# Tokens loaded by a matmul with a diagonal of norm factors, and 24 transposes of the identity as the tensor engine's first work

## The chip, the cores and the metric

The kernel runs on one core of a Trainium2 chip. Its engines are PE (matmul; PEld is the loading of the stationary operand), DVE (vector), ACT (activation), POOL and SP, which here only issues transfers. Each engine works through its own instructions strictly in the order in which they stand in the program. The metric is device time in microseconds of one launch, lower is better. The profile is one other execution, recorded by the hardware profiler.

## The reference

One step of a one-layer decoder over 1024 prompt tokens and 32 sample tokens (8 sequences of 4), width 1024, all in float32:

```python
def rmsnorm(x, g):
    return x * rsqrt(mean(x * x) + 1e-6) * g

def trunk_layer(x):
    x = x + 0.5 * rmsnorm(swiglu(rmsnorm(x, g[0])), g[1])       # FFN 1, inner width 2816
    h = rmsnorm(x, g[2]); z = h @ w_in                          # mLSTM q,k,v,o,i,f and window attention q,k,v
    u = concat(mlstm_heads(z), window_attention(z))
    x = x + rmsnorm(u @ w_out, g[3])
    x = x + 0.5 * rmsnorm(swiglu(rmsnorm(x, g[4])), g[5])       # FFN 2
```

The outputs are x for prompt and sample, and the new caches and states. The change concerns what comes before and at the first products of FFN 1: loading x, its norm and transposition.

## The kernel before, in words

**Tiling.** Tokens lie in four quarters q = 0 to 3, each 256 prompt tokens and 8 sample tokens (QW = 264 columns). The width of 1024 lies in eight blocks of 128 partitions, two to a tile (kp = 0 to 3). A float32 product is made of three matmuls in the type float32r: each operand is split into a high part (ACT rounds: `wh`, `Xh`) and a low part (DVE subtracts: `wl`, `Xl`), and high x high, high x low and low x high are summed. One such matmul has a 128x128 stationary operand and 264 moving columns.

**Stages.** FFN 1: the first pair of inner blocks goes plainly, quarter by quarter (PSUM tiles `pl`); the other ten pairs by a scheme with fewer products (`gu`) that needs sums and differences of the normed x of two quarters (function `sums`: tiles `xt`, then splits). Then the down projection (`pd`), first for quarters 0 and 1, then for 2 and 3; then the mix stage (`pz`, `pv`, `po`, `pw`), FFN 2 likewise, and the output.

**The start** (`load_x`). For each quarter SP loads 256 rows of tokens (`xt`, tokens on partitions). The sum of squares of each token (`jk`, `xss`) gives by `rstd`, ten small DVE instructions, the factor `r`. PE transposes the 16 blocks of 128x128 (`xT`, PE's transpose against the identity), ACT copies them to `xr`, POOL adds the 8 sample columns. A product of `r`, broadcast over 128 partitions, with the identity (`rb`) makes a row of factors `rrow` on all partitions. DVE multiplies `xr` by gain and `rrow` (`xb`, in `blocks`), and `Xh`/`Xl` are split from that. The unnormed `xr` is stashed in DRAM (`xs`) for the residual.

**The residual** (`post`). After the down projection of a pair of quarters the stashed tiles are loaded again (`x<-xs`). The sum of squares of the result is made by DVE (`sq`) and three matmuls with ones (`cs`); `rstd` and `rb` make the row `cr`; DVE multiplies and adds (`y`), ACT and DVE split for the next stage (`xh`, `xl`). PE goes on with the down projection of quarters 2 and 3 meanwhile. PSUM tiles for `cs` and `rb` share one single bank (BANKS `c=1`): `rb` of quarter 0 can be written only when DVE has read `cs` of quarter 1.

**Order.** The code spawns generators with due times in units of PE's estimated time (`Order`, the tables XW, XQ, PQ, SUMS), and a list scheduler then sets the order on each engine. So an edit at one place moves instructions at others.

## Time and profile before

| what | value |
|---|---|
| runs | 2020.64 us median of 3 (2015.86 to 2020.72) |
| the profiled execution: own time, span | 2019.21 us, 2017.4 us |
| mean granted TensorE clock in it | 0.996 |
| PE busy | 1986.5 us, 98% of the span |
| DVE, ACT, POOL busy | 1168.4, 874.9, 35.6 us |
| first `pl` matmul; first `gu` matmul | 17.01 us; 78.82 us after the span's start |

A row of a timeline has start, duration, engine, line, instruction, and in brackets how long the engine had been idle and what ended that. A row of instructions merged into one ("x4") has the time from the first start to the last end. Matmuls overlap, so what one costs is read from the distance of two starts, not from its duration. A float32 matmul (not float32r) shows as two records. The granted clock (PEclk) is a share of full speed.

### The profile page before, as it was taken

Reading aid. Unit: us, or ns where it says so; the run is one execution under the profiler, and the core shown is the slowest. Engines: PE = TensorE matmul, PEld = TensorE weight load, DVE = VectorE, ACT = ScalarE, POOL = GpSimd, SP = SyncE. Lnnn points to the kernel's source line nnn. Section 1 sums busy time; section 2 is a strip of 40 time slices with the busy share of each in tenths; the row PEclk is TensorE's granted clock in tenths of the full one; section 3 lists DMA queues with packets and bytes.
Section 4 is the critical chain, followed back from the end, with each engine's and each line's share of the span. In section 5 each row is a group of like instructions: output and inputs, shape, how many; then the busy total and the mean of one; then the engine's idle time right before and its main releaser. Section 6 shows DMA issues by size and latency. Waiting matters only on the chain.

```text
span 2017.4 us, 40347 instructions
## 1 busy us (share of the span) xinstructions
PE 1986.5 (98%) x16178; PEld 1942.6 (96%) x16178; DVE 1168.4 (58%) x2822; ACT 874.9 (43%) x2087; POOL 35.6 (2%) x166
## 2 busy tenths in 40 slices
PE   7999999999999999999999999999999999999997
PEld 7999999999999999987999999999999999999997
DVE  5855555557238436467556758785555556534764
ACT  6533333336336332346244655353333334533553
POOL 0000000000000001100101000000000000000000
PEclk9999999999999999999999999999999999999999
DMA  6122222226346343201214143322222223545773
GB/s 234 65 85 77 90 69 74 76 95 177 108 142 208 104 102 124 68 1 38 68 53 134 57 133 116 108 78 82 65 84 80 91 64 120 167 129 162 226 223 116
DMA packets 279690, 216.66 MB, mean 107 GB/s; under 512 B 21032, under 2 KB 252640, under 8 KB 279488
## 3 DMA queue, kind: packets, MB, share of 16 engines
q1 hardware_dynamic: 279504, 214.11, 35.0%
q8 instruction: 126, 2.06, 0.5%
q14 instruction: 60, 0.49, 0.1%
HBM read 172.39 MB, written 42.49 MB: 107 GB/s over the span
## 4 chain that ended last, share of the span: by engine, by line
PE 91%; DVE 3%; DMA 3%; ACT 2%; issue 1%; SPq 0%; DVEq 0%; ACTq 0%
PE gu L154 41%; PE pd L154 23%; PE pz L154 7%; PE pw L154 4%; PE pl L154 4%; PE pv L154 3%; PE po L154 2%; DMA raw<-ffn_w_down 2%; PE cs L154 1%; PE rb L154 1%; PE swo L154 1%; PE sws L154 1%; PE E L154 1%; ACT wh L196 1%; PE swp L151 1%
## 5 line engine op out<-in xcount | busy, mean ns | idle before, releaser
L154 PE MATMUL gu<-Xh,wh 128*128 128x264 f32 x2240 | 636.6, 284 | 0.0
L154 PE MATMUL gu<-Xl,wh 128*128 128x264 f32 x2240 | 636.0, 284 | 0.0
L154 PE MATMUL gu<-Xh,wl 128*128 128x264 f32 x2240 | 635.1, 284 | 0.0
L197 DVE TENSOR_TENSOR wl<-raw,wh 128x512 fp32r<-128x512 f32 x458 | 301.6, 670 | 384.3 <-ACT wh L196 376.5
L154 PE MATMUL pd<-hq,wh 128*128 128x264 f32 x2816 | 520.8, 286 | 0.1
L196 ACT CAST wh<-raw 128x512 fp32r<-128x512 f32 x458 | 270.1, 602 | 459.4 <-PE pd L154 193.2
L154 PEld LDWEIGHTS pd<-hq,wh 128*128 128x128 f32 x2816 | 437.8, 189 | 0.4 <-ACT yo L853 0.4
L154 PEld LDWEIGHTS gu<-Xh,wh 128*128 128x128 f32 x2240 | 421.1, 188 | 0.5 <-ACT sc L752 0.2
L154 PEld LDWEIGHTS gu<-Xh,wl 128*128 128x128 f32 x2240 | 421.6, 188 | 0.0
L154 PEld LDWEIGHTS gu<-Xl,wh 128*128 128x128 f32 x2240 | 421.3, 188 | 0.0
L154 PE MATMUL pd<-hq,wl 128*128 128x264 f32 x1408 | 401.1, 285 | 0.0
L154 PEld LDWEIGHTS pd<-hq,wl 128*128 128x128 f32 x1408 | 265.4, 188 | 0.2 <-DVE wl L197 0.2
L752 ACT COPY sc<-gu 128x264 f32<-128x264 f32 x240 | 91.0, 380 | 272.2 <-PE gu L154 268.0
L197 DVE TENSOR_TENSOR wl<-ws,wh 128x512 fp32r<-128x512 f32 x160 | 108.8, 690 | 87.6 <-ACT wh L196 84.7
L763 DVE TENSOR_TENSOR h<-gu,sc 128x264 f32<-128x264 f32 x120 | 51.8, 432 | 102.2 <-PE gu L154 83.3
L154 PE MATMUL pz<-xh,wh 128*128 128x264 f32 x352 | 102.3, 291 | 0.6 <-DVE z L1684 0.6
L154 PE MATMUL pz<-xh,wl 128*128 128x264 f32 x352 | 100.8, 286 | 0.0
L154 PE MATMUL pz<-xl,wh 128*128 128x264 f32 x352 | 100.5, 285 | 0.0
L196 ACT CAST wh<-ws 128x512 fp32r<-128x512 f32 x160 | 95.9, 623 | 4.1 <-PE pl L154 2.5
L764 ACT ACTIVATE h<-h 128x264 f32<-128x264 f32 x120 | 50.9, 425 | 106.5 <-DVE h L763 106.5
L769 DVE TENSOR_TENSOR sc<-gu,sc 128x264 f32<-128x264 f32 x120 | 51.6, 432 | 56.8 <-PE gu L154 51.4
L154 PE MATMUL pl<-Xh,wh 128*128 128x264 f32 x256 | 72.9, 299 | 3.3 <-ACT Xh L196 2.1
(368 smaller groups left out, 2969.6 us busy)
## 6 DMA issues: line engine op xcount, KB each, us to landing
raw<-ffn_w_down SPq DMA_DIRECT2D x80, 512.0 KB
raw<-ffn_w_gate SPq DMA_DIRECT2D x44, 512.0 KB
raw<-ffn_w_up SPq DMA_DIRECT2D x44, 512.0 KB
h<-h SPq DMA_DIRECT2D x80, 264.0 KB
hq<-h SPq DMA_DIRECT2D x160, 132.0 KB
raw<-ffn_w_down SPq DMA_DIRECT2D x40, 384.0 KB
x<-xs SPq DMA_DIRECT2D x48, 264.0 KB
raw<-w_in SPq DMA_DIRECT2D x21, 512.0 KB
```

Source lines behind the costliest of these rows:

```text
L151: K.nc.tensor.transpose(out, lhsT, rhs)
L154: K.nc.tensor.matmul(out, lhsT, rhs, start=start, stop=stop, **kw)
L196: K.nc.scalar.copy(hi, src)
L197: (eng or K.nc.vector).tensor_tensor(lo, src, hi.bitcast(F32), op=ALU.subtract)
L752: nc.scalar.copy(sc[n][:, g], ps)
L763: nc.vector.tensor_tensor(d, bk[tg, g], sc[n][:, g], op=ALU.add)
L764: nc.scalar.activation(d, d, AF.Silu)
L769: nc.vector.tensor_tensor(sc[n][:, g], src, sc[n][:, g], op=ALU.add)
```

## The change

- `load_x` no longer transposes against the identity. The factors `r` are computed first, DVE writes them as a diagonal (`diagonal`: identity times `r`, two of 128x128 for a quarter, in the tile `C`), and PE multiplies each block of tokens by the diagonal: transposition and norm in one float32 matmul. ACT makes `Xh` from PSUM with the gain as scale, DVE makes `Xl` from PSUM, ACT copies the normed x without gain (`xn`), and this is what is stashed.
- `rstd` gets its first guess by one instruction instead of two, and can also return the root `ru`. `rb` now broadcasts the root, and `post` of FFN 1 multiplies the reloaded tiles by it (16 new DVE instructions).
- `sums` makes the gained tiles `xb` (16 by DVE, 16 by ACT) that it used to find ready.
- The sample tokens come first and have their own norm; POOL copies 48 small pieces instead of 16.
- The first weights (`w0`) come in eight tiles of 256 KB between the tokens of quarters 0 and 1, and quarter 0's first products go over kp outermost (`first_pair`) with four PSUM tiles open.
- 24 transposes of the identity stand ahead on PE, one activation ahead on ACT.
- The copies of the attention caches from DRAM to DRAM become stores out of the tiles `kc` and `vc`, in `swa_sample`.

The core of the diff:

```diff
-XW = [2.0, 0.15, 0.2]
+XW = [2.0, 0.15, 4.0]
-XQ = [0, 0.0, 4.0, 10.0]
+WARM = 24
+XQ = [0, 3.0, 10.0, 20.0]
-SUMS = {(2, 0, 0): 0, (3, 0, 0): 1}
+SUMS = {1: {(1, 1, 1): 0, (3, 0, 0): 1}, 3: {(2, 0, 0): 0, (3, 0, 0): 1}}
...
+def first_loads(K):
+    K.xt = [slot(K, "xt")[0:32, 0:512] for _ in range(2)]
+    for i in range(2):
+        nc.sync.dma_start(K.xt[i], A["x_sample"].rearrange("b t d -> (b t) d")[:, i * 512:(i + 1) * 512])
+    load_tokens(K, 0)
+    for kp in range(4):
+        for mat, n in enumerate(("ffn_w_gate", "ffn_w_up")):
+            K.w0[kp, mat] = slot(K, "w0")[:, 0:512].rearrange("p (k m) -> p k m", k=2)
+            nc.sync.dma_start(K.w0[kp, mat], A[n][0, 0].rearrange("(k p) m -> p k m", p=P)[:, 2 * kp:2 * kp + 2, 0:256])
+    load_tokens(K, 1)
...
-    ri = r.bitcast(I32)
-    nc.vector.tensor_scalar(ri, v.bitcast(I32), 1, None, op0=ALU.arith_shift_right)
-    nc.vector.tensor_scalar(ri, ri, -1.0, float(0x5F3759DF), op0=ALU.mult, op1=ALU.add)
+    nc.vector.tensor_scalar(r.bitcast(I32), v.bitcast(I32), -0.5, float(0x5F3759DF), op0=ALU.mult, op1=ALU.add)
...
+    nc.vector.tensor_tensor(u, v, r, op=ALU.mult)
+    return r, u
...
+def diagonal(K, r, w, i):
+    d = K.C[0:w, i, 0:w]
+    K.last = K.nc.vector.tensor_scalar(d, K.ident[0:w, 0:w], r, None, op0=ALU.mult).ins
+    return d
...
-                pe(K, ps[:, (2 * i + j) * P:(2 * i + j + 1) * P], t[k // 4][:, (k % 4) * P:(k % 4) * P + P], K.ident,
-                   tr=True)
-        nc.scalar.copy(pair(x[kp])[:, :, 0:2 * P], ps.rearrange("p (a t) -> p a t", a=2))
+                pe(K, ps[:, (2 * i + j) * P:(2 * i + j + 1) * P], t[k // 4][:, (k % 4) * P:(k % 4) * P + P], dg[j])
+        for i in range(2):
+            nc.scalar.activation(h2[:, i, 0:2 * P], ps[:, i * 2 * P:(i + 1) * 2 * P], AF.Copy,
+                                 scale=K.gain[:, 2 * kp + i:2 * kp + i + 1])
+        for i in range(2):
+            ins = nc.vector.scalar_tensor_tensor(l2[:, i, 0:2 * P], ps[:, i * 2 * P:(i + 1) * 2 * P],
+                                                 K.gain[:, 2 * kp + i:2 * kp + i + 1], h2[:, i, 0:2 * P].bitcast(F32),
+                                                 op0=ALU.mult, op1=ALU.subtract)
+        nc.scalar.copy(x2[:, :, 0:2 * P], ps.rearrange("p (a t) -> p a t", a=2))
...
+        if phase == 1:
+            nc.vector.tensor_tensor(pair(t), pair(t), K.r[q].unsqueeze(1).to_broadcast([P, 2, QW]), op=ALU.mult)
...
+    nc.scalar.activation(warm, K.ones, AF.Silu)
+    for i in range(WARM):
+        nc.tensor.transpose(ps[:, 0:P], K.ident, K.ident)
```

What the scheduler makes of it stands below at three places. `xT` are the PSUM tiles of transposed tokens, `rb` the broadcast row; `xt`, and `raw` for quarter 1 now, hold loaded tokens; `C` holds the diagonals; numbers are the program's own.

PE at the start of the program, before: quarter 0's transposes need only the tokens, and the `rb` product comes ahead of the first `pl`.

```order
L151 MATMUL gps_94<-ident,graw_91 128x52
L151 MATMUL xT_146<-ident,xt_98 128x128
L151 MATMUL xT_146<-ident,xt_102 128x128
L151 MATMUL xT_146<-ident,xt_98 128x128
L151 MATMUL xT_146<-ident,xt_102 128x128
L151 MATMUL xsT_152<-ident,xt_106 128x32 x4
```

PE at the same place now:

```order
L158 MATMUL gps_132<-ident,graw_95 128x52
L1928 MATMUL warm_136<-ident 128x128 x24
L161 MATMUL xsT_186<-C,xt_98 128x32 x4
L161 MATMUL xsT_186<-C,xt_99 128x32 x4
L161 MATMUL xT_228<-C,xt_102 128x128
L161 MATMUL xT_228<-C,xt_104 128x128
```

The token blocks moved behind the diagonals, that is behind the sums of squares and `rstd`.

DVE before quarter 1's diagonals now (`ru_374` is its root, `C` the two diagonals; this had no counterpart before, since quarter 1's transposes waited for nothing of DVE's):

```order
L204 TENSOR_TENSOR wl_483<-w_15_122,wh_482 128x512
L273 TENSOR_SCALAR v_371<-xsn_369 128x2
L204 TENSOR_TENSOR wl_499<-w_16_124,wh_498 128x512
L274 TENSOR_SCALAR r_372<-v_371 128x2
L338 MEMSET xss_704 128x6
L409 SCALAR_TENSOR_TENSOR Xl_282<-xT_276,gain,Xh_281 128x256 x2
L276 TENSOR_TENSOR rt_373<-r_372,v_371 128x2
L277 TENSOR_TENSOR rt_373<-rt_373,r_372 128x2
L278 SCALAR_TENSOR_TENSOR ru_374<-rt_373 128x2
```

Here two weight splits and quarter 0's last `Xl` stand between the steps of quarter 1's `rstd`; six more rows follow before `C`. The rows of PE that need them stand in the midst of quarter 0's products:

```order
L161 MATMUL pl_338<-Xl_266,wh_352 128x264
L161 MATMUL rb_568<-ident,ru_374 128x128
L161 MATMUL xT_387<-C,raw_126 128x128
L161 MATMUL xT_387<-C,raw_127 128x128
L161 MATMUL xT_387<-C,raw_126 128x128
```

Whatever stands behind these rows on PE follows them in time, quarter 0's remaining products too.

DVE where `post` of quarters 0 and 1 begins, in the down projection of FFN 1, before (`sq` with one operand is the fold ahead of `cs`; `v` is the first step of `rstd`):

```order
L508 TENSOR_TENSOR sq_6367<-sq_6367,sq_7563 128x528
L197 TENSOR_TENSOR wl_7741<-raw_7738,wh_7740 128x512
L197 TENSOR_TENSOR wl_7745<-raw_7738,wh_7744 128x512
L244 TENSOR_TENSOR sq_6363<-sq_6363 128x264
L244 TENSOR_TENSOR sq_6367<-sq_6367 128x264
L197 TENSOR_TENSOR wl_7807<-raw_7804,wh_7806 128x512
L197 TENSOR_TENSOR wl_7811<-raw_7804,wh_7810 128x512
L265 TENSOR_SCALAR v_7851<-cs_7846 128x3
```

DVE at the same place now:

```order
L204 TENSOR_TENSOR wl_7875<-raw_7868,wh_7874 128x512
L516 TENSOR_TENSOR x_7917<-x_7917,rrow_439 128x528
L516 TENSOR_TENSOR x_7920<-x_7920,rrow_439 128x528
L516 TENSOR_TENSOR x_7923<-x_7923,rrow_439 128x528
L251 TENSOR_TENSOR sq_6493<-sq_6493 128x264
L204 TENSOR_TENSOR wl_7941<-raw_7938,wh_7940 128x512
L204 TENSOR_TENSOR wl_7945<-raw_7938,wh_7944 128x512
L516 TENSOR_TENSOR x_7972<-x_7972,rrow_572 128x528
L516 TENSOR_TENSOR x_7975<-x_7975,rrow_572 128x528
L516 TENSOR_TENSOR x_7978<-x_7978,rrow_572 128x528
L516 TENSOR_TENSOR x_7981<-x_7981,rrow_572 128x528
L273 TENSOR_SCALAR v_7989<-cs_7984 128x3
```

The new multiplications stand ahead of both folds and of `v`.

## The prediction

> **What bounds the kernel now.** I read the page's busy shares, then stretches of 5 us, the chain of waits and the timeline of the first 80 us, and then looked for every place where PE stands still.

> ```profile
> PE 1986.5 (98%) x16178; PEld 1942.6 (96%) x16178; DVE 1168.4 (58%) x2822; ACT 874.9 (43%) x2087; POOL 35.6 (2%) x166
> ...
> DMA  6122222226346343201214143322222223545773
> ```

> PE is the bound nearly everywhere. The start is the exception, and the stretches show where it ends (columns: stretch, its length, then busy time and instructions of each engine):

> ```profile
> 15.00:20.00 5.00, 3.25 (x13) 2.71 (x13) 4.33 (x8) 3.08 (x6) 0.00 (x0) 1.00 0.53 181
> 25.00:30.00 5.00, 4.44 (x33) 3.68 (x31) 3.55 (x15) 4.66 (x13) 0.00 (x0) 1.00 0.95 353
> 30.00:35.00 5.00, 5.00 (x38) 4.76 (x38) 3.86 (x9) 4.03 (x10) 0.00 (x0) 1.00 0.93 306
> ```

> From 30 us on PE has no gap, so a microsecond of PE work added before the `gu` stage costs a microsecond, and only what PE loses before 30 us can be won. The chain says when that stage begins:

> ```profile
> 66.88 11.94 PE pl L154 x96
> 78.82 41.22 PE gu L154 x338
> ```

> 78.82 us is the mark that the start is measured by. The timeline shows what precedes the first product:

> ```profile
> 7.92 0.63 ACT L317 ACTIVATE jk<-xt 128x512 f32<-128x512 f32 x1 [0.82 <-DMA xt<-x_prompt]
> 8.41 0.68 DVE L314 CUSTOM_DVE_ANT_0 jk<-xt 32x512 f32<-32x512 f32 x1 [1.42 <-DMA xt<-x_sample]
> ...
> 8.77 0.63 ACT L317 ACTIVATE jk<-xt 32x512 f32<-32x512 f32 x1
> ...
> 9.42 2.61 PE L151 MATMUL xT<-ident,xt 128*128 128x128 f32 x11
> 9.53 0.16 DVE L319 TENSOR_TENSOR xsn<-xss 128x3 f32<-128x3 f32 x1 [0.17 <-ACT jk L317]
> ...
> 9.93 0.17 DVE L267 TENSOR_SCALAR r<-v 128x3 int32<-128x3 int32 x1
> 10.14 0.17 DVE L268 TENSOR_SCALAR r<-r 128x3 int32<-128x3 int32 x1
> ...
> 13.11 1.23 PE L154 MATMUL rb<-ident,r 128*128 128x128 f32 x4 [1.08 <-DVE r L276]
> 14.26 0.59 PE L154 MATMUL rb<-ident,xtr 32*128 32x8 f32 x2
> ...
> 17.01 0.81 PE L154 MATMUL pl<-Xh,wh 128*128 128x264 f32 x2 [1.75 <-ACT Xh L196]
> ...
> 18.40 0.42 PE L154 MATMUL pl<-Xh,wh 128*128 128x264 f32 x1
> 18.62 0.42 PE L154 MATMUL pl<-Xl,wh 128*128 128x264 f32 x1
> ```

> Transposes run at 9.42 us, ahead of the factors; the first `pl` comes at 17.01 and repeats every 0.22 us.

> **The change, part by part.** Prices on PE, as distances of starts:

> ```profile
> 32.19 0.28 PE L154 MATMUL pl<-Xh,wl 128*128 128x264 f32 x1
> ...
> 37.21 0.28 PE L154 MATMUL pl<-Xh,wl 128*128 128x264 f32 x1
> 37.33 1.47 PE L151 MATMUL xT<-ident,xt 128*128 128x128 f32 x12
> 38.56 0.37 PE L154 MATMUL pl<-Xh,wh 128*128 128x264 f32 x1
> ...
> 41.99 0.60 PE L154 MATMUL rb<-ident,r 128*128 128x128 f32 x4
> ...
> 42.84 0.40 PE L154 MATMUL pl<-Xh,wh 128*128 128x264 f32 x1
> ```

> ```profile
> 1022.29 1.16 PE L154 MATMUL S<-z,z 128*128 128x128 f32 x8
> 1023.21 0.37 PE L154 MATMUL po<-xh,wh 128*128 128x264 f32 x1
> ```

> Between 32.19 and 37.21 lie 41 steps: 0.1224 us each, so the 384 `pl` take 47.0 us. A transpose is 1.23 / 12 = 0.103. A float32 matmul of 128x128, which `xT` becomes, is 0.92 / 4 = 0.23 (`S`, two records each). An `rb` group is 0.85.

> *When PE can begin.* Tokens of quarter 0 and the samples, 1.18 MB, have landed by 8.41 us; with the samples first, the last token tile takes their place. ACT then has two squares left (its row at 7.92 is followed by the next at 8.77, with another 0.7 behind), so the sum comes at about 9.85 instead of 9.53. Eleven small DVE steps at 0.2 (9.93 to 10.14) and the first diagonal, nothing between them, end at 12.3. The 24 transposes ahead and the activation cost nothing: even at 0.22 us they fit between the identity and 8 us, while the load runs; without that cover they would cost 2.5 us at 0.103.

> *PE's work from there.* 64 x 0.23 = 14.7, plus 47.0, plus 4 x 0.85 = 3.4: 65.1 us. Started at 12.3 and never waiting, `gu` would begin at 77.4: **-1.4 us**. The gain of beginning nearly five microseconds before 17.01 is eaten by 64 matmuls at more than twice a transpose's price.

> *The clock.* At 13.11 two float32 products need 1.15 us to the next row, against 0.54 or so later, and the `pl` at 18.40 step at 0.22: PE is at half speed until after 18.62, though transposes had filled it from 9.42 to 12.03. So I give the 24 no effect and charge 3 us at half speed from 12.3 on: **+1.5**. [...]

> Groups of one shape in `post`, with count, busy time and mean ns of one, give the prices on DVE:

> ```profile
> L466 DVE SCALAR_TENSOR_TENSOR xl<-y,gain,xh 128x264 fp32r<-128x264 f32 x32 | 15.0, 489 | 0.4 <-ACT xh L465 0.4
> L449 DVE TENSOR_TENSOR y<-y,x 128x528 f32<-128x528 f32 x16 | 11.1, 702 | 0.0
> ```

> *Waits.* Quarters 1 to 3 now need DVE before PE can transpose, and PE's order puts `rb` and `xT` of the next quarter into the midst of products. On ACT a kp costs two `Xh` (nearest row: the 489 ns above), a copy and a square of about 0.6 each, 2.2 us against PE's 2.9, so it keeps up. But DVE's steps to quarter 1's diagonal stand behind the last square (about 23 us), two splits and two `Xl`, and end at 27 to 28 by these prices, while PE arrives at 26.5. Quarter 2's root stands likewise behind the products' evacuation. I take 1 us for each of the three, between 0 (DVE on time) and 2: **+3.0**. The loads are hidden: w0 and quarter 1 bring 3.1 MB by about 19 us at 306 GB/s. Start in all: **+3.1**.

> *The 16 multiplications in `post`.* Here the one sizeable stop of PE outside the start lies:

> ```profile
> 631.00:632.00 1.00, 0.26 (x3) 0.04 (x1) 0.35 (x1) 0.93 (x2) 0.00 (x0) 1.00 1.10 333
> 632.00:633.00 1.00, 0.19 (x1) 0.20 (x2) 0.93 (x5) 0.00 (x0) 0.00 (x0) 1.00 0.05 13
> 633.00:634.00 1.00, 1.00 (x7) 1.00 (x7) 0.83 (x6) 0.00 (x0) 0.00 (x0) 0.57 0.09 27
> 634.00:635.00 1.00, 1.00 (x5) 1.00 (x6) 0.93 (x4) 0.38 (x1) 0.00 (x0) 0.50 0.97 293
> 636.00:637.00 1.00, 1.00 (x8) 1.00 (x8) 0.77 (x2) 1.00 (x2) 0.00 (x0) 0.72 0.00 0
> ```

> ```profile
> 624.01 0.77 DVE L244 TENSOR_TENSOR sq<-sq 128x264 f32<-128x264 f32 x2
> 627.71 1.30 DVE L197 TENSOR_TENSOR wl<-raw,wh 128x512 fp32r<-128x512 f32 x2 [2.93 <-ACT wh L196]
> ...
> 632.60 0.15 DVE L265 TENSOR_SCALAR v<-cs 128x3 f32<-128x3 f32 x1
> ```

> ```profile
> 625.00 0.72 PE L154 MATMUL cs<-ones,sq 128*128 128x1 f32 x6
> ...
> 629.70 0.72 PE L154 MATMUL cs<-ones,sq 128*128 128x1 f32 x6
> ...
> 632.81 1.16 PE L154 MATMUL rb<-ident,r 128*128 128x128 f32 x6 [1.55 <-DVE v L265]
> ```

> The multiplication is the form of `y<-y,x`: 0.70 there, some 0.62 from start to start. Four of them now stand ahead of the first fold (624.01): it ends near 626.9, and PE, at `cs` at 625.00, waits 1.9. Four more stand behind the splits that begin at 627.71 (to 629.0), so the second fold ends at 632.0 instead of 624.8, past PE's 629.70 + 1.9. Then the two `rstd` go interleaved, around two splits that wait for a load: root of quarter 0 near 635.4, `rb` at 635.5 instead of 632.81. **+2.7**, between 0 (the scheduler's estimate holds, and 2.9 idle us of DVE ahead of 627.71 take it) and 5 (all eight in series). The weights that DVE splits there are needed only some 10 us later.

> *Quarters 2 and 3.* The same eight at 755 to 775, where products of the mix stage cover them: +0.3, at most 2. *The rest*: `rstd` one step shorter, 0.2 us at the end and at 632: -0.4. The cache copies leave the start for a stage whose slices of the DMA row stand at 2 tenths: 0. Gains move from DVE (32 `xb`) to `sums` on DVE and ACT, due 15 us later: 0. POOL's 32 further copies: 0, it is 2% busy.

> **Sum**: 3.1 + 2.7 + 0.3 - 0.4 = +5.7 us on the profiled execution's 2019.21 us (span 2017.4): 2025, which is 4 us or 0.2% over the median 2020.64. About 0.3%, 6 us, is what a measurement of this kernel can tell from no change, so this is "the same", on the slow side.

> **Rivals.** (A) *DVE is on time*: the scheduler's order holds, neither diagonals nor folds make PE wait. For it: DVE stands idle 2.93 us ahead of 627.71. Against it: the folds stand behind three more multiplications in the queue. It decides whether quarter 1's diagonal is written before 26.5 us and the first fold before 625.0. Then the sum is 0.1 - 0.4: 2019. (B) *The stop at 631 vanishes*: if shifted orders take PE past it, 1.55 us of idle and the 1.7 lost at half clock go too: with A, 2015 or below. The `sq` rows speak against it. (C) *The waits put the clock down again.* The 1.55 us before 632.81 were enough for a granted clock of 0.57, 0.50 and 0.72 in the next stretches, 1.7 us lost. If each wait at a diagonal passes about 1.5 us, it costs 1.7 more: three of them, and a second such stop in `post`, add 7: 2032. [...] (D) *The 24 transposes do warm the clock*: 1.5 us less, 2023.5; the half speed behind 9.42's transposes speaks against it.

> **How the numbers follow.** The forecast, D with it, 0.5: 2025, own range 2021 to 2029. A 0.2, B 0.08, C 0.2, and 0.02 for something else. The range takes in A and most of C: 2016 to 2032. Faster by over 0.3% (below 2014.6): B and the tail of A, 0.1. Slower (above 2026.7): C and a third of the forecast, 0.38. The same: 0.52.

> **What would show it.** Right: the first `xT` matmul near 12.3, `gu` near 82, waits of PE on `C` or `ru` before quarters 1 to 3, `cs` and `rb` of `post` waiting on DVE with `rb` some 2.7 us later against the `pd` around it, and a half clock behind it. Wrong: `gu` before 78.8, `xT` at under 0.2 us each, or no stop of PE in `post`.

## The result, and the profile after

The changed kernel takes 2030.7 us (median of 5, 2023.79 to 2031.52) against 2016.18 us (median of 5, 2014.28 to 2020.72): 1.0055 times as long, with a 95% interval of 1.0032 to 1.0079. It is slower by some 11 us (0.55% of 2016). The forecast was 2025 us in 2016 to 2032, on the slow side; by its own bound of 0.3% the outcome is "slower", which had a chance of 0.38, and not "the same", which had 0.52.

Its profiled execution took 2030.7 us with a span of 2028.9. Both kernels were profiled a second time (spans 2012.9 before and 2025.6 after), and where the time went stands in the starts of each stage's first instruction in the four timelines:

| stage, to the first instruction of the next | before, two profiles | after, two profiles | difference of means |
|---|---|---|---|
| start, to the first `gu` | 78.7, 79.0 | 81.7, 81.5 | +2.8 |
| `gu` of FFN 1, to its first `pd` | 408.7, 408.9 | 411.5, 411.3 | +2.6 |
| `pd` of FFN 1 (`post` of quarters 0 and 1 in it) | 266.6, 265.3 | 266.8, 264.5 | -0.3 |
| mix stage (`post` of quarters 2 and 3 at its head) | 504.1, 504.0 | 507.4, 510.8 | +5.0 |
| `pl` of FFN 2, to its first `gu` | 49.3, 47.2 | 48.6, 50.1 | +1.1 |
| `gu` of FFN 2 | 418.1, 418.1 | 419.6, 419.2 | +1.3 |
| `pd` of FFN 2, to PE's last | 282.8, 281.5 | 285.1, 279.9 | +0.3 |

That is 12.8 us; what follows PE's last matmul is 0.7 shorter, so the spans differ by 12.1. The start is as forecast; the first down projection, where 2.7 were forecast, costs nothing; and some 10 us lie in stages that the forecast gave 0.3 to.

**The start.** PE's timeline of the first profile after:

```profile
2.92 5.38 PE L1928 MATMUL warm<-ident 128*128 128x128 f32 x24
8.23 2.11 PE L161 MATMUL xsT<-C,xt 32*128 32x32 f32 x16
13.15 5.49 PE L161 MATMUL xT<-C,xt 128*128 128x128 f32 x24 [2.81 <-DMA w<-ffn_w_up]
18.29 0.72 PE L161 MATMUL pl<-Xh,wh 128*128 128x264 f32 x2
...
28.62 2.84 PE L161 MATMUL xT<-C,raw 128*128 128x128 f32 x24
```

The first `xT` comes at 13.15 (12.74 in the second profile). Its 12 products take 5.49 us, 0.46 each, while the same number at 28.62 takes 2.84, 0.24 each: behind the 24 transposes the products ran at half speed (granted clock 0.50 from 12 to 18 us, 1.00 from 28 to 32). The wait of 2.81 is put down to a weight load, which these products do not read; the diagonals are written just then, as DVE's timeline of the same profile shows:

```profile
10.76 0.16 DVE L350 TENSOR_TENSOR xsn<-xss 128x2 f32<-128x2 f32 x1 [1.34 <-ACT jk L348]
...
12.82 0.48 DVE L357 TENSOR_SCALAR C<-ident,r 128x128 f32<-128x128 f32 x2
...
27.61 0.48 DVE L357 TENSOR_SCALAR C<-ident,r 128x128 f32<-128x128 f32 x2
40.88 0.48 DVE L357 TENSOR_SCALAR C<-ident,r 128x128 f32<-128x128 f32 x2
50.79 0.48 DVE L357 TENSOR_SCALAR C<-ident,r 128x128 f32<-128x128 f32 x2
```

The diagonals of quarters 1 to 3 end at 28.1, 41.4 and 51.3. PE comes to them at 28.6, 41.4 and 51.3: no wait above 0.3 us stands between 18.3 us and `gu`.

**The waits of PE**, as the view of waits sums them (us in all, times, longest), first profile after:

```profile
PE cs L161 <- DVE sq L251: 3.4, 3, 1.5
...
PE pz L161 <- DVE z L1840: 2.3, 2, 1.8
...
PE kcT L158 <- DMA kc<-cache_swa_k: 1.2, 1, 1.2
```

(`sq` ahead of `cs` is the fold; `z` is what DVE makes of the mix stage's first products `pz`; `kcT` are transposes of cached keys.) In the first down projection the `cs` of quarter 0 waits for its fold, and `rb` no longer waits:

```profile
632.12 0.80 PE L161 MATMUL cs<-ones,sq 128*128 128x1 f32 x6 [1.31 <-DVE sq L251]
638.41 0.72 PE L161 MATMUL cs<-ones,sq 128*128 128x1 f32 x6
640.18 0.78 PE L161 MATMUL rb<-ident,r 128*128 128x128 f32 x6
```

So the 1.55 ahead of `rb` went and a new wait of 1.31 came, with a half-clock stretch behind it as in the first profile before (granted clock 0.80, 0.50 and 0.85 in the three stretches of 2 us from 632). In the second profiles the waits are 0.62 ahead of `cs` and 1.15 ahead of `rb`; behind the latter no half clock came (granted 1.00 from 630 to 636).

Why `rb` no longer waits stands on DVE. `cs` and `rb` share one PSUM bank, so `rb` of quarter 0 needs `v` of quarter 1 to have read `cs`. Before, two weight splits stood between, and they waited for ACT and so for a load; `v` followed them at 632.60 and `rb` at 632.81. After, the last split comes ahead of quarter 1's `cs`, and `v` waits for PE; quarter 0's root is ready 0.2 us ahead of `rb`. Before, then after, first profiles:

```profile
631.65 1.03 DVE L197 TENSOR_TENSOR wl<-raw,wh 128x512 fp32r<-128x512 f32 x2 [0.80 <-ACT wh L196]
632.60 0.15 DVE L265 TENSOR_SCALAR v<-cs 128x3 f32<-128x3 f32 x1
```

```profile
637.83 0.42 DVE L204 TENSOR_TENSOR wl<-raw,wh 128x256 fp32r<-128x256 f32 x1 [0.98 <-ACT wh L203]
...
639.17 0.16 DVE L273 TENSOR_SCALAR v<-cs 128x3 f32<-128x3 f32 x1 [0.65 <-PE cs L161]
```

**The stop in the mix stage.** `post` of quarter 3 puts its multiplications ahead of the `z` that PE waits for. DVE and PE, second profile after:

```profile
770.57 1.94 DVE L516 TENSOR_TENSOR x<-x,rrow 128x528 f32<-128x528 f32 x3
772.43 0.42 DVE L1840 SCALAR_TENSOR_TENSOR z<-pz,rrow 128x264 f32<-128x264 f32 x1
772.77 0.70 DVE L516 TENSOR_TENSOR x<-x,rrow 128x528 f32<-128x528 f32 x1
...
778.72 0.42 DVE L1840 SCALAR_TENSOR_TENSOR z<-pz,rrow 128x264 f32<-128x264 f32 x1
```

```profile
779.19 0.39 PE L161 MATMUL pz<-xh,wh 128*128 128x264 f32 x1 [1.86 <-DVE z L1840]
```

The stretches behind it, of the first profile after and then of the second (length; busy time and instructions of PE, PEld, DVE, ACT and POOL; granted clock; DMA share and GB/s):

```profile
780.00:782.00 2.00, 0.49 (x4) 0.49 (x5) 2.00 (x8) 0.62 (x2) 0.47 (x1) 1.00 0.11 41
782.00:784.00 2.00, 2.00 (x19) 2.00 (x18) 2.00 (x7) 0.26 (x1) 0.00 (x0) 1.00 0.00 0
```

```profile
780.00:782.00 2.00, 2.00 (x11) 2.00 (x11) 1.97 (x8) 0.58 (x2) 0.14 (x1) 0.50 0.00 0
```

The same stop (1.83 and 1.86 us) is followed by full speed once (granted clock 1.00) and by half speed the other time (0.50).

**The stores that hold back a load.** SP's queue in the second profile after, what ended SP's own waits there, and PE behind it:

```profile
976.66 3.40 SPq L1376 DMA_DIRECT2D o_s_swa_v<-vc  x1
982.84 0.40 SPq L1373 DMA_DIRECT2D kc<-cache_swa_k  x1
```

```profile
SPq L1373 <- DMA o_s_swa_k<-kc: 2.7, 1, 2.7
```

```profile
988.20 1.09 PE L158 MATMUL kcT<-ident,kc 128*128 128x128 f32 x4 [1.62 <-DMA kc<-cache_swa_k]
```

The store of `vc` holds SP's queue for 3.40 us (why was not shown); the second load of `kc` stands behind it, and waits 2.7 us more for the store of the first `kc`.

**A slower step with no wait in it.** In 270 us of `gu` in FFN 1 PE is busy throughout, and the number of matmuls in brackets is smaller after. First the two profiles of before, which read alike but for the DMA columns, then the line that both profiles of after give:

```profile
210.00:480.00 270.00, 270.00 (x2226) 1.00 0.29 88
```

```profile
210.00:480.00 270.00, 270.00 (x2226) 1.00 0.28 87
```

```profile
210.00:480.00 270.00, 270.00 (x2216) 1.00 0.27 84
```

The step, the time from one matmul to the next, is 0.1213 us before and 0.1218 after (x2216 in both profiles), at a granted clock of 1.00. Over 3360 `gu` that is 1.8 us; in FFN 2 (2965 against 2958 matmuls in the 360 us from 1340) it is 1.0.

### The profile page after: what moved, and what is told of

The parts are those of the page before. It is cut to its first block, busy times and chain, and to the rows that moved or that the text cites. A ratio compares the mean times of both kernels' runs of the same rounds, so it can differ in the third digit from the quotient of the medians.

```text
span 2028.9 us, 40652 instructions
## 1 busy us (share of the span) xinstructions
PE 1998.4 (98%) x16274; PEld 1957.4 (96%) x16274; DVE 1173.6 (58%) x2832; ACT 880.3 (43%) x2120; POOL 43.3 (2%) x200
## 4 chain that ended last, share of the span: by engine, by line
PE 90%; DVE 4%; DMA 3%; ACT 2%; issue 1%; SPq 0%; DVEq 0%; ACTq 0%
PE gu L161 40%; PE pd L161 22%; PE pz L161 6%; PE pw L161 5%; PE pl L161 4%; PE pv L161 3%; PE po L161 2%; DMA raw<-ffn_w_down 2%; PE xT L161 1%; PE cs L161 1%; PE swo L161 1%; PE sws L161 1%; PE rb L161 1%; PE E L161 1%; DVE y L529 1%
## 5 line engine op out<-in xcount | busy, mean ns | idle before, releaser
L204 DVE TENSOR_TENSOR wl<-raw,wh 128x512 fp32r<-128x512 f32 x450 | 296.0, 669 | 384.5 <-ACT wh L203 381.4
L203 ACT CAST wh<-raw 128x512 fp32r<-128x512 f32 x450 | 265.1, 601 | 453.6 <-PE pd L161 198.3
L161 PE MATMUL pw<-uh,wh 128*128 128x264 f32 x256 | 73.8, 288 | 0.0
```

What stands on the lines that cost most here:

```text
L161: K.nc.tensor.matmul(out, lhsT, rhs, start=start, stop=stop, **kw)
L203: K.nc.scalar.copy(hi, src)
L204: (eng or K.nc.vector).tensor_tensor(lo, src, hi.bitcast(F32), op=ALU.subtract)
```

## The experiments

Theories at the outset: (T) the losses belong to parts of the change, the products with diagonals, the multiplications in `post`, the stores of the caches, each with a price of its own; (O) they belong to the new order of all engines, so that taking a part out only moves them; (C) the half clock makes them. "First `gu`" is the mark of the start.

**1 and 2. Both kernels once more.**

> The kernel before once more, unchanged, for one look. In the two profiles at hand the 3360 gu products of FFN 1 follow each other every 0.1214 us before and every 0.1219 us after, 1.7 us over the stage, without any wait in it. If that pitch belongs to the execution, this profile may show anything between 0.1212 and 0.1222; if it belongs to the kernel, it shows 0.1214 again (0.0002 either way). The first gu stands at 78.8 us, within 0.5.

> The changed kernel once more, unchanged, for one look on the same chip. If the pitch of gu belongs to the kernel: 0.1219 again, 0.0004 or more above the run of before beside it. If it belongs to the execution: the two pitches differ otherwise, or not at all. Everything that is a wait should come back: first gu at 81.8, PE idle ahead of gu near 98 us (0.4), ahead of cs at 632 (1.3), ahead of pz at 781 (1.8), ahead of kcT at 988 (1.2), each within 0.3 us.

Measured: 2015.0 and 2027.38 us. The step of `gu` came back to a thousandth in each (x2226 and x2216): it belongs to the kernel and not to the execution. The stops at 780 (1.86) and at `kcT` came back too, the latter longer than expected (1.62); the stop ahead of `cs` at 632 was 0.62 instead of 1.31, and the one at 98 fell to 0.28.

**3. No transposes ahead.**

```diff
-WARM = 24
+WARM = 0
```

> The 24 transposes of the identity are left out. My theory: they neither cost nor bring anything: xT still runs at half speed, 0.45 us a product, from 13.15 us to about 18.6, and gu begins at 81.8, within 0.3. The rival, that they count for the clock and shorten the half-clock stretch: xT at half speed for longer, gu at 82.5 to 84.

Measured: first `gu` at 81.74, `xT` at 12.95, taking 4.49 us for the 12 products instead of 5.49. The transposes brought nothing that one execution can show: run 6 has them and took 4.58. The time was 2034.76 us, 4 to 7 above the kernel with them, but not for the start: 13 us at half speed behind a wait of 1.47 us for a state's load account for it (stretch, length, PE busy, granted clock):

```profile
1112.00:1114.00 2.00, 0.93 (x11) 1.00 1.10 326
1114.00:1116.00 2.00, 1.61 (x21) 0.83 0.97 259
1116.00:1128.00 12.00, 12.00 (x66) 0.50 0.55 163
```

**4 and 8. Real products ahead instead of transposes.** In 4, 24 float32 products of the identity, and 8 more behind `xsT`; in 8, 16 and 8, and quarter 1's squares on ACT held behind the second pair of `Xh`.

```diff
-        nc.tensor.transpose(ps[:, 0:P], K.ident, K.ident)
+        nc.tensor.matmul(ps[:, 0:P], K.ident, K.ident, start=True, stop=True)
...
+        pw = bank(K, "warm", "a")
+        for i in range(8):
+            nc.tensor.matmul(pw[:, 0:P], K.ident, K.ident, start=True, stop=True)
```

> The 24 transposes become 24 plain float32 products of the identity with itself, and 8 more stand behind the sample tokens' products, so that PE is at work on products from 2.9 to about 12.9 us. My theory: the half clock from 13.15 to 18.6 goes, xT takes 0.23 us each instead of 0.45, and q0's products begin when ACT has its first Xh, near 16.5 instead of 18.3: gu at about 80.1, 1.7 us earlier (79.1 if ACT keeps up wholly). A ratio to before of about 1.0047 against 1.0055. Rival: the clock is not what holds the start, the operands' splits on ACT and DVE are: gu stays at 81.3 to 82, and the idle time moves ahead of pl. Second rival: PE's full work at the start counts for nothing because the gaps remain: xT at 0.45 us as before.

> As e4_real_warm, with 16 products ahead and 8 behind the sample tokens' (e4's 24 ended 2.4 us after the transposes), and the squares of quarter 1 held behind ACT's second pair of Xh (in e4 they had slipped ahead of the first and waited for their load, so Xh came at 19.5 instead of 15.4). My theory: the half clock costs the start 1 to 2 us and no more, because ACT's first Xh comes at 16: xT from 12.8 at 0.235 us each, first pl at 16.5 to 17.2, gu at 79.8 to 80.8 instead of 81.6. Rival: ACT's queue of eight weight casts ahead of Xh holds all: gu at 81.3 or later in spite of the full clock.

Measured: 4 took 1.0123 times before (1.0106 to 1.0140), 8 took 2039.66 us. Both did away with the half speed at `xT` (its 12 products took 2.84 and 2.94 us instead of 5.49), and both lost. PE's timeline of 8:

```profile
10.24 2.05 PE L401 MATMUL warm<-ident 128*128 128x128 f32 x16
13.22 2.94 PE L161 MATMUL xT<-C,xt 128*128 128x128 f32 x24 [0.93 <-DVE C L357]
17.11 0.36 PE L161 MATMUL pl<-Xh,wh 128*128 128x264 f32 x1 [0.95 <-POOL Xh L425]
...
42.58 0.46 PE L161 MATMUL rb<-ident,ru 128*128 128x128 f32 x2 [2.57 <-DVE ru L285]
```

`xT` runs at 0.245 us, near the 0.237 at 28.62 in the changed kernel, and `pl` begins 1.2 us sooner than at 18.29. But PE now reaches quarter 2 before its root, which stands on DVE behind a weight difference that waits for its load:

```profile
37.98 0.15 DVE L280 SCALAR_TENSOR_TENSOR rt<-r,v 128x2 f32<-128x2 f32 x1
40.58 0.69 DVE L731 TENSOR_TENSOR ws<-raw,raw 128x512 f32<-128x512 f32 x1 [2.46 <-DMA raw<-ffn_w_gate]
41.19 0.15 DVE L281 TENSOR_TENSOR rt<-rt,r 128x2 f32<-128x2 f32 x1
```

The load came late, too: the same `ws` started at 39.11 in the changed kernel, 1.5 us sooner than here. With the stop of 2.57 `gu` began at 85.03. Of the 9 to 12 us that run 8 is slower, only 3.4 lie in the start; some 7 lie in the last `pd` (289 to PE's last, against 285 and 280), where PE once stood 2.80 us. In 4, squares of quarter 1 had slipped ahead of quarter 0's first `Xh` on ACT and waited for their load, so that `Xh` came at 19.54 instead of 15.75; PE stood 2.93 us ahead of `pl`, and behind that `pl` stepped at half speed (0.22 us from 21.39 on): `gu` at 89.03. The theory that the half clock alone holds 1 to 2 us of the start was not borne out in either; what the start would give at full clock in an unchanged order was not got.

**5. The token blocks transposed again.**

```diff
-t[k // 4][:, (k % 4) * P:(k % 4) * P + P], dg[j])
+t[k // 4][:, (k % 4) * P:(k % 4) * P + P], K.ident, tr=True)
```

> The changed kernel with its 64 token blocks transposed against the identity again instead of multiplied by the diagonals; the diagonals are still written, and nothing else is changed (the norm factor is left out of x that way). My theory: the price of the products is the main thing that the start pays. 48 blocks at full clock cost 0.105 us instead of 0.235 (6.2 us less), 16 at half clock some 0.22 instead of 0.45, of which 1.5 to 2 are won since ACT's first Xh holds the products at 16.5: gu begins at 73.5 to 76 instead of 81.6, and the ratio to before is about 1.002, 6 to 8 us less than the changed kernel. Rival: the diagonals' wait and ACT's queue hold the start, and the price hides under them: gu at 79 or later.

Measured: first `gu` at 74.02, 7.5 us sooner, as the price of the products said. But the time was 2028.35 us, 1.0064 times before (1.0047 to 1.0081), and the span 2025.9 against 2028.9 and 2025.6: of 7.5 us at most some 2 arrived. By the stages `gu` of FFN 1 took 412.6 (+1.2 on the mean of after), its `pd` 267.7 (+2.0), the mix stage 510.5 (+1.3), the last `pd` 284.9 (+2.4). Two `cs` in the first `pd` waited 0.99 and 1.42, and between `gu` and the output five stops had a half clock behind them, against three and four in the two profiles of after (in the first the granted clock fell to 0.50 behind 632, 1298 and 1946). This speaks for (O) beside (T).

**6. No multiplication in `post`.**

```diff
-            nc.vector.tensor_tensor(pair(t), pair(t), K.r[q].unsqueeze(1).to_broadcast([P, 2, QW]), op=ALU.mult)
```

> The changed kernel without the 16 multiplications of x by the root in post (the residual keeps its normed x). My theory: for quarters 0 and 1 they cost nothing net, since their wait ahead of cs (0.6 to 1.3 us) stands where the rb wait (1.2 to 1.6) stood before, so the first down projection still takes 264.5 to 267 us; for quarters 2 and 3 they stand ahead of z on DVE and are the reason of the stop of 1.85 us ahead of pz at 780: that stop falls to 0.6 or less, and from first pz to first pv it is 66.0 to 66.5 us instead of 68.0 and 69.9. Rival: the order of the list scheduler, not the multiplications, makes that stop: it stays at 1.5 or more, 68 us or more.

Measured: 2023.27 us. The stop at 780 is gone: first `pz` to first `pv` takes 65.5 us, and the mix stage 503.7, as before the change. The `kcT` wait fell to 0.2 as well, though the stores are still there (the one of `vc` holds the queue for 3.27). In the first down projection `cs` no longer waits, and the wait is back at `rb`, with the two splits ahead of `v` again:

```profile
637.16 1.45 PE L161 MATMUL rb<-ident,r 128*128 128x128 f32 x6 [2.36 <-DVE v L273]
```

```profile
636.01 1.03 DVE L204 TENSOR_TENSOR wl<-raw,wh 128x512 fp32r<-128x512 f32 x2 [3.04 <-ACT wh L203]
636.95 0.15 DVE L273 TENSOR_SCALAR v<-cs 128x3 f32<-128x3 f32 x1
```

That `pd` took 268.6, 2.9 more than with the multiplications and above the 267 expected; in run 12, again without them, it took 264.5. Over all profiles here, the seven with the multiplications on DVE have a wait at the `cs` of quarter 0 (0.62 to 2.05) and none at `rb`, and the six without them have one at `rb` (0.43 to 2.36) and none at `cs`. The stage took 266.6 on average in the seven and 266.0 in the six. So for quarters 0 and 1 the multiplications cost next to nothing; for quarters 2 and 3 they cost about 2.5 to 4.4 (65.5 against 68.0 and 69.9 to the first `pv`).

Part of this run's 2023.27 is not the edit's. Up to `gu` the order of all engines is that of the changed kernel, yet `gu` began at 79.79, 1.8 sooner, because quarter 0's diagonal came sooner (`xT` at 12.14 instead of 13.15) and its 12 products took 4.58 us instead of 5.49:

```profile
12.14 4.58 PE L161 MATMUL xT<-C,xt 128*128 128x128 f32 x24 [1.65 <-DVE C L357]
```

**7 and 9. The cache copies.** 7 is the change with the two DRAM to DRAM copies back; the scheduler sets them into the start, as in the kernel before. 9 is the kernel before with the same copies held in `swa_sample`:

```diff
+        last = nc.sync.dma_start(vc.rearrange("p (b f) -> p b f", b=4), cv[:, 4 * hf:4 * hf + 4])
+        if hf == 1:
+            with K.tc.issue_after(last.ins):
+                # the two DRAM to DRAM copies
```

> The changed kernel with the cache copies as they were, two DRAM to DRAM transfers at the head of swa_sample instead of four stores out of kc and vc. My theory: the store of vc waits 3.4 us in SP's queue for its own load, and the second load of kc stands behind it, so kcT waits 1.2 and 1.6 us: without the stores that wait is gone, and from first pv to first po it takes 200.5 us as before instead of 201.9 and 203.7. Rival: kc comes late for lack of a free tile or bandwidth: the wait stays at 1 us or more.

> The kernel before, with one thing from the change alone: the two DRAM to DRAM cache copies (1 MB) leave the start. They are not turned into stores but held in SP's queue behind the last load of kc and vc, so nothing waits for them. My theory: in the kernel before they stand ahead of the first load of ffn_w_up and of quarter 2's tokens, and are the cause of the wait for wh at 23.8 us (1.1 and 1.95 us in two profiles): that wait falls below 0.5, gu begins at 76 to 77.8 instead of 78.7 to 79.0, nothing is lost in the mix stage (first pv to first po 200.5), ratio 0.9985 to 0.9995. Rival: the load of ffn_w_up takes its six microseconds anyway, gu at 78.5 or later and ratio 1.000; or the new order brings a stop elsewhere, ratio above 1.001.

Measured in 7: the `kcT` wait is gone and first `pv` to first `po` takes 200.5 us, as expected. But the first `gu` came at 87.96, 6.4 later, and the time was 2033.03 us. The copies stand at 17.95 in SP's queue, the next load of `ffn_w_gate` goes at 37.62 instead of 33.38, and later ACT's gains for `sums` stand ahead of the `h` that PE waits for:

```profile
72.51 1.73 ACT L470 ACTIVATE xb<-xn,gain 128x264 f32<-128x264 f32 x4
74.14 0.37 ACT L838 ACTIVATE h<-pl 128x264 f32<-128x264 f32 x1
```

```profile
74.66 0.36 PE L161 MATMUL pl<-Xh,wh 128*128 128x264 f32 x1 [1.92 <-ACT h L838]
```

This stop and the half clock behind it (`pl` at 0.22 us) make some 3.6 of the 6.4 us; the rest was not traced. Since the edit took both stores away, it does not tell which of the two held the load of `kc`.

Measured in 9: 1.0027 times before (1.0016 to 1.0038). The theory fell, and the second rival held. The wait for `wh` at 23.8 did go, but waits for the next tokens, for `h` and for `h` again took its place (1.21 us at 24.33, 1.30 at 39.75, 1.00 at 69.03): `gu` at 80.89.

**10. One unused tile.** The kernel before with one slot taken at the start and never used; the order of PE, DVE, ACT and SP is the same word for word.

```diff
+    K.nc.gpsimd.memset(slot(K, "pad")[:, 0:1], 0.0)
```

> The kernel before with one tile slot taken at the start and never used: every engine's order stays the same word for word, but 3160 of the 6720 moving operands of gu lie in another slot. If the pitch of gu depends on where the tiles lie: a pitch 0.0002 or more away from 0.1214 (FFN 1) or 0.1215 (FFN 2), in either direction, reproducible only by the layout. If not: 0.1214 and 0.1215 again, and the pitch has another cause (order, or what the other engines do meanwhile).

Measured, in the rows of the same two stretches as above:

```profile
210.00:480.00 270.00, 270.00 (x2219) 1.00 0.28 86
1340.00:1700.00 360.00, 360.00 (x2968) 1.00 0.27 83
```

x2219 in FFN 1 against 2226 twice, a step of 0.1217 instead of 0.1213, and 2968 in FFN 2 against 2965 twice: the step moves by 0.3% in the one and by 0.1% the other way in the other. With the order held, the place of the tiles is the difference between the two programs. Which places are slow was not found: the 1216 `gu` of FFN 1 of which neither the moving operand nor the next one's had moved slowed most (from 0.1215 to 0.1226), so it is not their own address alone. That the placement is what slowed `gu` in the changed kernel is the likely reading, not shown.

**11. Both repairs.** The change with the copies held as in 9, and the 16 multiplications on POOL.

> The changed kernel with two repairs: the cache copies as DRAM to DRAM transfers held behind the last load of kc and vc, and the 16 multiplications of post on POOL instead of DVE. My theory: the kcT wait (1.2 to 1.6) goes, the stop ahead of pz at 780 (1.85) falls to 0.6 or less as without the multiplications, the start stays at gu 79.8 to 81.8: from first pz to first pl 504 us as in the kernel before instead of 507.4 and 510.8, ratio about 1.003 instead of 1.0055 to 1.006. Rival: POOL needs 2 us or more for a multiplication that DVE does in 0.7, x comes late for y, and the stop moves there: pz to pl 507 or more.

Measured: 1.0083 times before (1.0064 to 1.0101), worse than the change itself; the rival held, though at a lower price than its 2 us. Group of POOL's multiplications (count, busy time, mean ns):

```profile
L516 POOL TENSOR_TENSOR x<-x,rrow 128x528 f32<-128x528 f32 x16 | 24.5, 1559 | 731.6 <-PE pd L161 602.6 <-DMA x<-xs 129.1
```

1.56 us for what DVE does in 0.7, so the stops grew: `cs` 2.61, `rb` 2.90 and 1.40, `pz` 2.41. From first `pz` to first `pl` it took 510.6 us. The `kcT` wait went.

**12. Both priced parts out.**

> The changed kernel with both parts out that its own experiments priced: token blocks transposed against the identity (e5; the norm factor is left out of x) and no multiplication in post (e6). What remains of the change is the order of loads, the stores of the caches, the work of sums, and the new order of all engines. My theory: the two prices add: gu at 73.5 to 75 (e5: 74.0), from first pz to first pl 503.5 to 505 us (e6: 503.7), the pitch of gu 0.1216 to 0.1221, and in all 2027.3 less 7.6 and 5 plus what the first down projection gives back (2), so 2015 to 2019, ratio 0.9995 to 1.002. Rival: what is won at the start is given back by later stops whatever one takes out, as in e5, where 7.6 us at the start left only 2 in the time: ratio 1.003 or more.

Measured: 1.0009 times before (0.9997 to 1.0020), `gu` at 74.48, the stop at 780 gone (`pz` to `pv` 65.5), `kcT` still waiting 1.28, x2215 in the 270 us of `gu`. The mix stage took 507.1, not 503.5 to 505. The two parts together are worth 1.0055 less 1.0009, 9 us: most of the loss, so (T) holds for the two together. For one alone it is weaker: without the products the ratio did not fall (run 5), and run 6 is one execution. Against the start of before the remaining kernel has won 4.3 us and gives them back in `gu` (412.8, +4.0), the `kcT` wait and elsewhere, which is (O).

No version beat the kernel before.

## Why the prediction was right, and where not

- **Range and sign**: 2030.7 lies in 2016 to 2032, on the slow side as forecast, near the upper end. The sum of +5.7 was half of what the runs showed (11 to 12).
- **Start, +3.1**: +2.8, but not by its terms. PE began at 12.7 to 13.2 (12.3 forecast), since the sum of squares was complete at 10.4 and 10.8 and not at 9.85. The half clock cost 2.7 (5.49 less 2.84, 1.5 forecast). The three waits at diagonals, +3.0, did not come: quarter 1's diagonal was written when forecast (27 to 28), but PE arrived at 28.4 instead of 26.5, since it had begun later and slower. The errors cancelled, and some 0.9 us are left unexplained. That the sums agree is luck: in runs 6 and 11, with the same order up to `gu`, it began at 79.79 and 82.29, so one execution differs from the next by nearly as much as was forecast. Run 8 shows such a wait: with PE sooner and a load later, PE stood 2.57 us for quarter 2's root.
- **Price of `xT`, 0.23 and 64 of them**: right (0.237 at full speed; run 5 gave 7.5 us back).
- **`post` of quarters 0 and 1, +2.7**: wrong, -0.3. The wait at `cs` came (1.31 and 0.62; 1.9 forecast). The failed step is that a wait at `rb` was kept behind it, with the two `rstd` "around two splits that wait for a load". That load was the cause of the old wait (1.55 and 1.15), and in the new order the splits were done by about the time quarter 1's `cs` was, so `v` followed `cs` within 0.4 us and `rb` did not wait. Run 6 shows the other side: with the splits behind again, PE waited 2.36 at `rb`.
- **Quarters 2 and 3, +0.3, "products of the mix stage cover them"**: wrong. The cover failed because DVE also reads `pz` out of PSUM (`z`), and PE waits for that: 1.85 us and, in one profile of two, a half clock (granted 0.50 from 780 to 782). First `pz` to first `pv` grew by 2.0 and 3.8; run 6 took that away.
- **Cache copies, 0**: wrong both ways. Where they went they hold a load behind stores (1.2 to 1.6 us of PE's time, but 0.2 in run 6); putting them back into the new start cost 6.4, with the order that came of it (run 7), while taking them out of the old start won nothing (run 9).
- **Gains to `sums`, 0**: a stop of 0.42 us at 98 in one profile, 0.28 in the other.
- **Not forecast**: the slower step of `gu`, 1.8 and 1.0 us, a quarter of the loss.
- **Rivals**: (A) no wait of PE above 0.3 us came from a diagonal of quarters 1 to 3, but the folds did make it wait. (B) The stop at 631 vanished from `rb`, but another came at `cs`. (C) The half clock came behind some waits of 1.3 to 1.9 us (granted 0.50 behind 1.31 at 632, and in the second profile behind 1.86 at 779 and 1.62 at `kcT`) and not behind others (1.00 behind 1.83 at 781); its price fitted (1.7 us by the granted clock from 632 to 638), its certainty did not. (D) fell: `xT` ran at half speed behind the 24 transposes (0.46 us a product, against 0.24 at 28.62).

What stood ahead of the first 12 products shows in their time: 5.49 us behind 24 transposes (4.58 in run 6), 4.49 behind none (run 3), 2.94 behind 24 real products (run 8) and 2.84 behind 32 (run 4). The rows of the work ahead differ, too: the 24 transposes follow each other every 0.213 us to the last, while in run 8 the 32 records of the first 16 products take 5.51 us, where 0.213 for each would make 6.8, and the 16 records of the next 8 take 2.05, 0.13 each.

## What to carry to other kernels

Work that is moved to an engine with half its time idle is not free at the place where that engine also releases the bound engine's buffers (here DVE, 58% busy before the change, and 1.83 and 1.86 us of PE's time at `pz`): price it by what stands behind it in that queue. When a wait is predicted at a new place, ask what caused the old one next to it, and whether that cause still stands behind the new one, before adding both. And in a kernel at 98% of its bound whose order and layout are set by a scheduler, every edit tried here moved stops of PE and tiles' places, by several microseconds in all, so a gain at one mark (7.5 us here) must be looked for in the whole time.
